# Twenty-four small score products of the compressed branch, handed out by threes

## The chip, the cores and the metric

The kernel runs on one core of a Trainium2 chip. The core has five engines with an instruction queue each: TensorE (PE in the rows; its weight loads are shown as PEld), VectorE (DVE), ScalarE (ACT), GpSimd (POOL) and SyncE (SP), which issues most transfers. Each engine takes its queue in order, and semaphores hold an instruction until what it needs is there. The metric is the time of one execution on the device in microseconds (us), the median over several runs.

## The reference

One layer of a decoder trunk for 256 tokens of width 2048, in float32. After a norm, one projection feeds three mixers: dilated window attention (12 heads, group "a"), block attention (8 heads, "b") and a sparse mixer (12 heads in 3 key groups, "c"). Their 32 head outputs go through an output projection and a residual; then a gated convolution FFN (width 5632) and a last norm. The change is in the sparse mixer's compressed branch, where each of the 12 heads scores 15 compressed keys:

```python
def chunk(c):
    ...
    s_c = jnp.einsum('bkgqe,bkne->bkgqn', qc, kc)
    p_c, _ = masked_softmax(s_c, cmp_end[None, :] <= t[:, None])
    o_c = jnp.einsum('bkgqn,bkne->bkgqe', p_c.astype(v_cmp.dtype), vc)
    ...
    return g[..., 0:1] * o_c + g[..., 1:2] * o_s + g[..., 2:3] * o_w
```

`o_s` and `o_w` are the selected and the window branch. With 256 tokens every block is selected, so both are causal attention over all keys, with keys and values of their own.

## The kernel before

**Main products.** Weights come from memory in chunks of 128 x 1024. ScalarE casts a chunk to a high part `wh` (L129), VectorE forms the rest `wl` (L131), and TensorE multiplies both with the split input: `wh` times 512 columns (L184), `wl` times 256 columns (L188). A chunk is 16 such main products. Raw chunks have 4 buffers, `wh` and `wl` 5 each. A unit of the projection (128 outputs, 32 main products, two chunks) fills one PSUM bank of the pool `mm`, which has three. When a unit is done, `evac` gathers it: ScalarE copies one half of the bank to `low` (L205), VectorE adds the other (L206), which frees the bank. `low` has one buffer (`FULL_BUFS = 1`); it is free again when the unit's outputs are written. For a query unit these are two query tiles (L346 on ScalarE, L347 on VectorE), and query tiles have 12 buffers.

**Order of the units.** First the twelve units of group c's keys and queries and its values (`cq0` to `cq5` are the queries, two heads each), then group a: `aq00, ak00, aq10, ak10, aq20, ak20`, then its values (three products to a piece, L406 to L408), and so on to group b. The six `cq` units fill all 12 query buffers.

**Side work.** The attention runs beside the main products as a list of Python generators. The main loop calls `step()` once after each chunk and twice after every second one; each call runs the first generator to its next `yield`. When `cq5` is issued, `c_attention` is started: first `cmp_attention` (the compressed branch), then `pipeline` over 24 head instances (12 heads, selected and window branch; the order is head 0, head 1 selected, head 0, head 1 window, then heads 2 and 3). One step of the pipeline turns an earlier instance's probabilities (three transposes, L585 to L587), scores one instance (three products, L532 and L534, into one of the two banks of the pool `sc`) and issues its softmax: a bias add (L546) and two reductions with a minimum (L548) on VectorE, which free the bank, two exponentials on ScalarE (L549), a factor (L552, L553, L557) and two scalings on VectorE (L580, L581). A query tile is free when both instances that use it are scored.

**The compressed branch** (L481 to L521): 12 products of 32 columns for each half of the tokens, into one `sc` bank each (L491); VectorE adds mask and low part (L493, L494), takes the minimum and subtracts it (L497, L498); ScalarE exponentiates (L500); then mask, sum, reciprocal, gate and scaling on VectorE (L503 to L511), and four transposes (L515, L516).

**The final order** on each engine is set when the program is built: a scheduler walks all instructions with a model of their durations, takes the ready one that stands earliest in the program's text, and hands out buffers. So the place of a `yield` sets which instructions stand earlier, and the built order is fixed for the chip.

Of the kernel before, what the change touches and what calls it, by code (L numbers as in the profile page):

```python
# [92 lines left out]
def trunk(ctx, tc, xT, wfm, wtm, wout, wup, wdown, wlast, gT, w1, w2, pe, relT, convp, onehot, maskc, cmask, vbmask, out, out_t):  # L93
# [115 lines left out]
    with tc.tile_pool(name="sc", bufs=2, space=bass.MemoryType.PSUM) as scp, \  # L209
# [107 lines left out]
        def turned(t):  # L317

            return t.rearrange("p (b c) -> p b c", c=P)[:, :, ::-1]
# [162 lines left out]
        def cmp_attention():  # L482
            ge = st["gate"].rearrange("p t g -> p (t g)")
            ps = ptp.tile([P, 512], F32, name="pt")
            T.matmul(ps[:, :72], flip, ge, start=True, stop=True)
            V.tensor_copy(ge, ps[:, :72])
            sm = rp.tile([P, 2, 12, 16], F32, name="sb")
            for tt in range(2):
                sps = scp.tile([P, 512], F32, name="sc")
                for h in range(12):  # L490
                    T.matmul(sps[:, h * 32:h * 32 + 32], qs[f"cq{h // 2}", h % 2][:, tt * P:(tt + 1) * P], cmp["k"][:, h // 4, :], start=True, stop=True)  # L491
                s3 = sps[:, :384].rearrange("p (h n) -> p h n", n=32)
                V.tensor_tensor(sm[:, tt], s3[:, :, :16], cm[:, 0, tt, :].unsqueeze(1).to_broadcast([P, 12, 16]), ALU.add)  # L493
                V.tensor_tensor(sm[:, tt], s3[:, :, 16:], sm[:, tt], ALU.add)  # L494
            sm2 = sm.rearrange("p t h n -> p (t h) n")
            mn = ap.tile([P, 24], F32, name="cmn")
            V.tensor_reduce(mn, sm2, AX.X, ALU.min)  # L497
            V.tensor_tensor(sm2, sm2, mn.unsqueeze(2).to_broadcast([P, 24, 16]), ALU.subtract)  # L498
            e = rp.tile([P, 2, 12, 16], F32, name="p", bufs=PROB_BUFS)
            A.activation(e, sm, AF.Exp, scale=-1.0)  # L500
            yield
            for tt in range(2):
                V.tensor_tensor(e[:, tt], e[:, tt], cm[:, 1, tt, :].unsqueeze(1).to_broadcast([P, 12, 16]), ALU.mult)  # L503
            e2 = e.rearrange("p t h n -> p (t h) n")
            den = ap.tile([P, 24], F32, name="cden")
            V.tensor_reduce(den, e2, AX.X, ALU.add)
            V.tensor_scalar_max(den, den, 1e-30)
            V.reciprocal(den, den)
            V.tensor_tensor(den.rearrange("p (t h) -> p t h", t=2), den.rearrange("p (t h) -> p t h", t=2),
                            st["gate"].rearrange("p t (h b) -> p t h b", b=3)[:, :, :, 0], ALU.mult)  # L510
            V.tensor_tensor(e2, e2, den.unsqueeze(2).to_broadcast([P, 24, 16]), ALU.mult)  # L511
            yield
            tp = ptp.tile([P, 512], F32, name="pt")
            for tt in range(2):
                T.transpose(tp[:, tt * P:(tt + 1) * P], e[:, tt, :8].rearrange("p h n -> p (h n)"), ident)  # L515
                T.transpose(tp[:64, 256 + tt * P:256 + (tt + 1) * P], e[:, tt, 8:].rearrange("p h n -> p (h n)"), ident)  # L516
            pc = cmp["pc"] = [cmp["big"][:, 6:8, :].rearrange("p a b -> p (a b)"), ap.tile([64, S], F32, name="pc1")]
            A.copy(pc[0].rearrange("p (b c) -> p b c", c=P), turned(tp[:, :S]))
            A.copy(pc[1].rearrange("p (b c) -> p b c", c=P), turned(tp[:64, S:2 * S]))
            yield  # L520
# [126 lines left out]
        def c_attention():  # L647
            insts = []
            for p in range(6):
                kv = p // 2  # L650
                for br, (grp, base) in enumerate((("s", 0), ("w", 192))):
                    for hf in range(2):
                        i = Inst(f"cq{p}", ("c", br, kv), "c", base + kv * HD, 20 + 2 * p + hf, grp, hf)
                        i.done = 10 + p if grp == "w" else None
                        insts.append(i)
            yield from cmp_attention()
            yield from pipeline(insts, 2, lambda j: scale(insts[j]))
# [335 lines left out]
```

## Time and profile before

| | us |
|---|---|
| median of 3 runs | 1161.84 (1161.62 to 1163.25) |
| the profiled execution | 1162.18 |
| its span in the profile | 1160.2 |
| TensorE busy | 1146.8 (99% of the span) |
| VectorE busy | 859.1 (74%) |
| ScalarE busy | 684.5 (59%) |
| granted TensorE clock, mean over the run | 0.998 of full speed |

The span runs from the first to the last instruction that the profile shows; the execution's time has 2.0 us around it. Busy shares are averages over stages with different limits: VectorE is far busier in the attention stage (the first 350 us) than later. A matmul's row shows its start and a modelled end, which overlaps the next one's start; how long it holds TensorE is read from start to start.

### The profile page before, as it was taken

The numbers are of one execution on the slowest core, as the hardware profiler recorded it, in microseconds if no ns is written. First come the engines' busy times: TensorE is split into PE (matmuls) and PEld (weight loads), VectorE is DVE, ScalarE is ACT, GpSimd is POOL, SyncE is SP. The second block draws the span as 40 slices with busy tenths as digits, with TensorE's granted clock in tenths as the row PEclk, the third lists the DMA queues.
The fourth block names the chain that finished last, engine by engine and source line by source line (L and its number), as shares of the span: only waits on it lengthen the run. The fifth ranks groups of instructions, "written<-read, shape, count | busy, mean of one in ns | idle before, by whom it ended". The sixth has DMA issues, their size and how long they took to land.

```text
span 1160.2 us, 18818 instructions
## 1 busy us (share of the span) xinstructions
PE 1146.8 (99%) x6931; PEld 1016.7 (88%) x6931; DVE 859.1 (74%) x1666; ACT 684.5 (59%) x1181; POOL 28.8 (2%) x61
## 2 busy tenths in 40 slices
PE   8999999999999999999999999999999999999997
PEld 6898998988888998888888888888888888888897
DVE  6877977877786878888888888888888555544565
ACT  7674786867764657655565555656556544444452
POOL 2000000100000000000000000000000100000000
PEclk9999999999999999999999999999999999999999
DMA  9765545565466755555555555555556866656612
GB/s 305 257 189 174 139 169 153 158 201 164 142 176 174 214 195 184 193 186 189 192 187 192 186 190 192 188 192 185 193 188 190 308 212 173 191 183 186 195 55 73
DMA packets 67276, 215.06 MB, mean 185 GB/s; under 512 B 7648, under 2 KB 11888, under 8 KB 67184
## 3 DMA queue, kind: packets, MB, share of 16 engines
q1 hardware_dynamic: 63200, 204.15, 54.7%
q0 software_dynamic: 3008, 8.86, 3.1%
q8 instruction: 55, 0.90, 0.3%
q10 hardware_dynamic: 976, 0.85, 0.2%
q14 instruction: 37, 0.30, 0.1%
HBM read 211.68 MB, written 2.15 MB: 184 GB/s over the span
## 4 chain that ended last, share of the span: by engine, by line
PE 98%; DMA 1%; DVE 0%; ACT 0%; SPq 0%; issue 0%; DVEq 0%
PE up L184 40%; PE up L188 21%; PE mm L184 13%; PE mm L188 6%; PE mm L407 2%; PE mm L406 2%; PE mm L408 2%; PE up L892 1%; PE up L894 1%; PE up L893 1%; PE sc L534 1%; PE o L611 1%; DMA gx<-in_xT_dram 1%; PE mm L195 1%; PE mm L193 1%; PE mm L194 1%
## 5 line engine op out<-in xcount | busy, mean ns | idle before, releaser
L131 DVE TENSOR_TENSOR wl<-raw,wh 128x1024 fp32r<-128x1024 f32 (+3 forms) x398 | 464.1, 1168 | 178.0 <-ACT wh L129 168.0
L129 ACT CAST wh<-raw 128x1024 fp32r<-128x1024 f32 (+3 forms) x398 | 400.5, 1008 | 263.2 <-PE up L184 177.4
L184 PE MATMUL up<-xx,wh 128*128 128x512 f32 x1408 | 483.8, 393 | 0.0
L188 PE MATMUL up<-xx,wl 128*128 128x256 f32 x1408 | 379.5, 280 | 0.0
L184 PEld LDWEIGHTS up<-xx,wh 128*128 128x128 f32 x1408 | 257.9, 188 | 50.9
L188 PEld LDWEIGHTS up<-xx,wl 128*128 128x128 f32 x1408 | 265.2, 188 | 7.9
L184 PE MATMUL up<-aa,wh 128*128 128x512 f32 x616 | 215.6, 394 | 0.0
L188 PE MATMUL up<-aa,wl 128*128 128x256 f32 x616 | 171.9, 283 | 0.0
L184 PE MATMUL mm<-xx,wh 128*128 128x512 f32 x448 | 158.6, 396 | 1.0 <-ACT wh L129 1.0
L184 PEld LDWEIGHTS up<-aa,wh 128*128 128x128 f32 x616 | 114.9, 188 | 25.4
L188 PE MATMUL mm<-xx,wl 128*128 128x256 f32 x448 | 122.9, 283 | 3.4 <-DVE wl L131 3.4
L188 PEld LDWEIGHTS up<-aa,wl 128*128 128x128 f32 x616 | 115.8, 188 | 1.2
L205 ACT COPY low<-up 128x256 f32<-128x256 f32 x88 | 32.8, 373 | 125.8 <-PE up L184 125.8
L184 PEld LDWEIGHTS mm<-xx,wh 128*128 128x128 f32 x448 | 82.9, 188 | 16.5 <-ACT wh L129 1.3
L188 PEld LDWEIGHTS mm<-xx,wl 128*128 128x128 f32 x448 | 84.3, 188 | 6.5 <-DVE wl L131 4.3
L206 DVE TENSOR_TENSOR low<-up,low 128x256 f32<-128x256 f32 x88 | 37.4, 425 | 55.8 <-ACT low L205 55.6
L184 PE MATMUL mm<-oo,wh 128*128 128x512 f32 x192 | 67.0, 395 | 0.0
L789 ACT ACTIVATE acc<-u,cw 128x256 f32<-128x256 f32 x88 | 53.2, 604 | 3.2 <-DVE u L787 0.6
L188 PE MATMUL mm<-oo,wl 128*128 128x256 f32 x192 | 52.1, 283 | 0.0
L407 PE MATMUL mm<-wh,xx 128*128 128x384 f32 (+2 forms) x128 | 46.3, 362 | 0.0
L406 PE MATMUL mm<-wh,xx 128*128 128x384 f32 (+2 forms) x128 | 46.3, 362 | 0.0
L408 PE MATMUL mm<-wl,xx 128*128 128x384 f32 (+2 forms) x128 | 45.5, 359 | 0.0
(250 smaller groups left out, 1305.8 us busy)
## 6 DMA issues: line engine op xcount, KB each, us to landing
raw<-in_wup_dram SPq DMA_DIRECT2D x176, 512.0 KB, 4.4
raw<-in_wdown_dram SPq DMA_DIRECT2D x70, 512.0 KB, 4.1
raw<-in_wfm_dram SPq DMA_DIRECT2D x62, 512.0 KB, 4.6
raw<-in_wo_dram SPq DMA_DIRECT2D x32, 384.0 KB, 3.1
raw<-in_wtm_dram SPq DMA_DIRECT2D x16, 384.0 KB, 3.3
bias<-table POOLq DMA_DIRECT2D x32, 128.0 KB, 3.8
raw<-in_wtm_dram SPq DMA_DIRECT2D x8, 512.0 KB, 4.5
raw<-in_wo_dram SPq DMA_DIRECT2D x8, 512.0 KB, 4.4
```

Of the source, the lines that this page charges most:

```text
L129: A.copy(wh[:, :n], raw[:, :n])
L131: V.tensor_tensor(wl[:, :n], raw[:, :n], wh[:, :n].bitcast(F32), ALU.subtract)
L184: T.matmul(ps, a, m.rearrange("p c s -> p (c s)"), start=start, stop=stop)
L188: T.matmul(ps[:, :S], b, m[:, 0, :], start=False, stop=False)
L193: T.matmul(ps[:, :S], a, m[:, 0, :], start=start, stop=False)
L194: T.matmul(ps[:, :S], a, m[:, 1, :], start=False, stop=False)
L205: A.copy(t, ps[:, S:])
L206: V.tensor_tensor(t, ps[:, :S], t, ALU.add)
L406: T.matmul(pss[tt][:, :n], xx[:, kt, 0, ts], a, start=kt == 0, stop=False)
L407: T.matmul(pss[tt][:, :n], xx[:, kt, 1, ts], a, start=False, stop=False)
L408: T.matmul(pss[tt][:, :n], xx[:, kt, 0, ts], b, start=False, stop=kt == NK - 1)
L789: A.activation(acc, u[:, 2:], AF.Identity, bias=cw[:, n, 3:4], scale=cw[:, n, 0:1])
```

## The change

Inside the loop over the 12 heads of a half, `cmp_attention` now yields after every third product. It had three yields before it ended and has eleven now, so each later step of `c_attention`, and of the generators behind it in the list, is run eight steps later.

```diff
                 for h in range(12):
                     T.matmul(sps[:, h * 32:h * 32 + 32], qs[f"cq{h // 2}", h % 2][:, tt * P:(tt + 1) * P], cmp["k"][:, h // 4, :], start=True, stop=True)
+                    if h % 3 == 2:
+                        yield
                 s3 = sps[:, :384].rearrange("p (h n) -> p h n", n=32)
```

The instructions are the same ones on every engine; the two added lines shift the line numbers behind L491 by two. The order on POOL and SP is the same. On TensorE, VectorE and ScalarE the order differs from the first small product to the scores of group b, about 900 main products further on.

TensorE's queue from the end of the first chunk of `aq00`. Before:

```order
L485 MATMUL pt<-gate,flip 128x72
L491 MATMUL sc<-kc,q 128x32 x20
L188 MATMUL mm<-xx,wl 128x256
...
L491 MATMUL sc<-kc,q 128x32 x4
L188 MATMUL mm<-xx,wl 128x256
```

and with the change:

```order
L485 MATMUL pt<-gate,flip 128x72
L491 MATMUL sc<-kc,q 128x32 x3
L188 MATMUL mm<-xx,wl 128x256
...
L491 MATMUL sc<-kc,q 128x32 x6
L184 MATMUL mm<-xx,wh 128x512
...
L491 MATMUL sc<-kc,q 128x32 x3
L188 MATMUL mm<-xx,wl 128x256
```

Before, 20 small products stand together and 4 more come 22 main products later. Now there are six groups (3, 6, 3, 6, 3, 3) with 16 main products between one and the next.

TensorE's queue around the end of `ak10`, the 112th main product after the first small one. `q_854` and `q_857` are the two query tiles of `cq0`, `q_909` and `q_912` those of `cq1`. Before, the first two scores (of `cq0`'s selected branch) stand 58 main products ahead of this place, and the next ones stand so (`mm_1505` is `ak10`, `mm_1643` is `aq20`):

```order
L532 MATMUL sc_1340<-k_545,q_854 128x256
...
L188 MATMUL mm_1505<-xx_83,wl_1378 128x256
L532 MATMUL sc_1404<-k_545,q_857 128x256
...
L515 MATMUL pt_1227<-ident_68,p_1195 128x128
...
L585 MATMUL pt_1334<-ident_68,p_1279 128x128
...
L184 MATMUL mm_1505<-xx_83,wh_1425 128x512
L532 MATMUL sc_1451<-k_510,q_909 128x256
...
L532 MATMUL sc_1476<-k_510,q_912 128x256
L534 MATMUL sc_1476<-k_510,q_912 128x256 x2
L184 MATMUL mm_1643<-xx_83,wh_1508 128x512
```

With the change all of them stand between `ak10` (`mm_1343`) and `aq20` (`mm_1441`):

```order
L184 MATMUL mm_1343<-xx_83,wh_1303 128x512
L534 MATMUL sc_1408<-k_510,q_854 128x256
...
L534 MATMUL sc_1464<-k_510,q_857 128x256
...
L534 MATMUL sc_1513<-k_545,q_854 128x256
...
L534 MATMUL sc_1540<-k_545,q_857 128x256
...
L534 MATMUL sc_1598<-k_510,q_909 128x256
...
L517 MATMUL pt_1396<-ident_68,p_1331 128x128
...
L587 MATMUL pt_1507<-ident_68,p_1415 128x128
...
L534 MATMUL sc_1645<-k_510,q_912 128x256
...
L184 MATMUL mm_1441<-xx_83,wh_1346 128x512
```

Six scores, the four transposes of the compressed branch and one turn (three transposes) now follow one another without a main product between them. Further on, after `ak20` (64 main products later), there is a second such row: four scores and three turns between `ak20` and the first product of group a's values.

VectorE's queue from the first of these scores' bias add to the gather of `ak00`. Before (`low_1359` is `ak00`'s gather):

```order
L546 TENSOR_TENSOR sb_1276<-sc_1272,bias_1268 128x128
...
L131 TENSOR_TENSOR wl_1559<-raw_1555,wh_1557 128x1024
...
L131 TENSOR_TENSOR wl_1648<-raw_1644,wh_1646 128x1024
...
L347 SCALAR_TENSOR_TENSOR q_1239<-low_1235,q_1239 64x256
...
L131 TENSOR_TENSOR wl_1695<-raw_1691,wh_1693 128x1024
L206 TENSOR_TENSOR low_1359<-mm_1245,low_1359 128x256
```

With the change (`low_1261` is `ak00`'s gather, whose end the first product of `aq20` waits for):

```order
L548 TENSOR_TENSOR sb_1412<-sc_1408,bias_1404 128x128
...
L131 TENSOR_TENSOR wl_1574<-raw_1570,wh_1572 128x768
...
L347 SCALAR_TENSOR_TENSOR q_1198<-low_1194,q_1198 64x256
...
L347 SCALAR_TENSOR_TENSOR q_1201<-low_1194,q_1201 64x256
...
L550 ISA sb_1544,nm_1545<-sc_1540,bias_1406 128x256
...
L206 TENSOR_TENSOR low_1261<-mm_1204,low_1261 128x256
```

The three chunk splits that stood between the first bias add and the gather of `ak00` are ahead of the bias add now, and the next split (768 wide) stands there instead. The bias adds and minima of four instances and the two query writes of `aq00` stand between them as before.

## Rows read from the trace of the kernel before

**Rows 1.** The page: TensorE's busy line, and the chain that ended last by engine

```profile
PE 1146.8 (99%) x6931; PEld 1016.7 (88%) x6931; DVE 859.1 (74%) x1666; ACT 684.5 (59%) x1181; POOL 28.8 (2%) x61
PE 98%; DMA 1%; DVE 0%; ACT 0%; SPq 0%; issue 0%; DVEq 0%
```

**Rows 2.** Busy us in one stretch: PE, PEld, DVE, ACT, POOL; clock, DMA share, GB/s

```profile
117.00:130.00 13.00, 13.00 (x85) 11.72 (x84) 12.48 (x45) 8.37 (x22) 1.08 (x2) 1.00 0.46 136
```

**Rows 3.** Waits of ScalarE from 116 to 160: total us, times, longest

```profile
ACT q L346 <- PE sc L534: 2.0, 4, 0.7
```

**Rows 4.** Timeline, TensorE, the small products: start us, duration us, instruction

```profile
104.82 2.38 PE L491 MATMUL sc<-kc,q 128*128 128x32 f32 x20
...
110.99 0.51 PE L491 MATMUL sc<-kc,q 128*128 128x32 f32 x4
...
111.35 0.36 PE L188 MATMUL mm<-xx,wl 128*128 128x256 f32 x1
```

**Rows 5.** Timeline, TensorE, the first scores, transposes and the start of `aq20`

```profile
117.01 0.28 PE L532 MATMUL sc<-k,q 128*128 128x256 f32 x1
...
117.72 0.28 PE L188 MATMUL mm<-xx,wl 128*128 128x256 f32 x1
...
123.65 0.28 PE L532 MATMUL sc<-k,q 128*128 128x256 f32 x1
...
128.39 0.27 PE L585 MATMUL pt<-ident,p 128*128 128x128 f32 x1
128.50 0.27 PE L586 MATMUL pt<-ident,p 128*128 128x128 f32 x1
...
130.34 0.39 PE L184 MATMUL mm<-xx,wh 128*128 128x512 f32 x1
```

**Rows 6.** Timeline, ScalarE, a query write and a gather's copy

```profile
124.20 0.42 ACT L346 ACTIVATE q<-low 64x256 fp32r<-64x256 f32 x1 [0.70 <-PE sc L534]
...
127.14 0.37 ACT L205 COPY low<-mm 128x256 f32<-128x256 f32 x1
```

**Rows 7.** Timeline, VectorE, from the first bias add to `ak00`'s gather

```profile
118.39 0.28 DVE L546 TENSOR_TENSOR sb<-sc,bias 128x128 f32<-128x128 f32 x1
118.59 0.61 DVE L503 TENSOR_TENSOR p<-p,cm 128x192 f32<-128x192 f32 x2
...
120.97 1.22 DVE L131 TENSOR_TENSOR wl<-raw,wh 128x1024 fp32r<-128x1024 f32 x1
122.10 0.30 DVE L508 RECIPROCAL cden<-cden 128x24 f32<-128x24 f32 x1
...
125.14 0.28 DVE L580 TENSOR_SCALAR p<-p,f 128x128 f32<-128x128 f32 x1
...
125.59 0.28 DVE L546 TENSOR_TENSOR sb<-sc,bias 128x128 f32<-128x128 f32 x1
125.91 0.42 DVE L347 SCALAR_TENSOR_TENSOR q<-low,q 64x256 fp32r<-64x256 f32 x1
...
129.39 0.42 DVE L206 TENSOR_TENSOR low<-mm,low 128x256 f32<-128x256 f32 x1
```

**Rows 8.** Timeline, VectorE, from a later bias add to the gathers of `ak10` and `aq20`

```profile
138.03 0.28 DVE L546 TENSOR_TENSOR sb<-sc,bias 128x128 f32<-128x128 f32 x1
...
141.81 0.94 DVE L131 TENSOR_TENSOR wl<-raw,wh 128x768 fp32r<-128x768 f32 x1
142.66 0.29 DVE L548 CUSTOM_DVE_ANT_0 sb<-sc,sb 128x128 f32<-128x128 f32 x1
...
143.29 0.42 DVE L206 TENSOR_TENSOR low<-mm,low 128x256 f32<-128x256 f32 x1
...
148.22 0.42 DVE L206 TENSOR_TENSOR low<-mm,low 128x256 f32<-128x256 f32 x1 [0.30 <-ACT low L205]
```

**Rows 9.** Busy time in two stretches with TensorE mostly idle (columns as in Rows 2)

```profile
10.00:12.00 2.00, 0.53 (x3) 0.19 (x1) 0.79 (x2) 1.73 (x3) 0.00 (x0) 1.00 1.02 392
1153.00:1156.00 3.00, 0.49 (x2) 0.30 (x2) 2.54 (x9) 0.20 (x1) 0.00 (x0) 0.79 0.16 54
```

## The prediction, made before the changed kernel ran

> **What bounds the kernel now.** I read the page first: the reader is to see that TensorE is busy 99% of the span and that the chain that ended last runs through it for 98% [rows 1]. So time that TensorE gains or loses in the middle of the program moves the end by as much, unless something later gives it back. I read the stretch around the edit next, by engine: TensorE is busy for all of its 13.00 us, and VectorE for 12.48 of them [rows 2]. There VectorE has next to no room, and whatever TensorE must wait for on VectorE will take the full length of VectorE's queue. The waits name the place: ScalarE already waits four times, 2.0 us in all, for scores before it can write group a's query tiles [rows 3], since the twelve query buffers hold group c's queries until these are scored. Last I read the timelines of the three engines for durations.
>
> **What the change moves.** The number of instructions stays. The small products come apart, and every later step of the attention comes eight steps later. The main loop calls three steps for two chunks, so that is 16/3 chunks or some 15 us (32 main products, two chunks, took 5.66: 111.35 to 117.01) [rows 4, 5]. The unit `aq00` can't write its queries, and `low` stays taken, until `cq0`'s four scores are done; `ak00` can't be gathered until `low` is free; and with three `mm` banks, `aq20` has none until `ak00` is gathered. Before, `ak00`'s gather starts at 129.39 and takes 0.42, and `aq20`'s first product starts at 130.34: 0.53 us of room [rows 5, 7]. Eight steps are far more. The built order shows it: the scores of `cq0` now stand behind the last product that has a bank, and TensorE must run six scores, four transposes and a turn in a row, at VectorE's pace, before `aq20`.
>
> **The small products.** Twenty took 2.38, 0.119 each with the modelled end, and the group of four took 0.36 until the next main product, 0.09 each [rows 4]: the first weight load of a group lies under the main product ahead of it, the others don't. There are four groups more, so I take 4 x 0.09 = 0.36 off, rounded to -0.3. The bounds: if all 24 loads hid and the products cost nothing, -2.7 (2.38 + 0.36); if breaking the row cost as much as it saves, +0.3.
>
> [...]
>
> **The first stall** (between `ak10` and `aq20`). Four pieces of TensorE's own work lie in it and are needed anyway, so they are no loss: two scores take 0.71 (117.01 to 117.72), so a score takes 0.355 and six take 2.13; a transpose takes 0.11 (128.39 to 128.50), so four and three take 0.77 [rows 5]. Sum 2.90.
>
> Its length is VectorE's queue. From a score's start to the next engine's start there passed 0.55 (123.65 to 124.20, an idle ScalarE that waited for it) [rows 5, 6]. Then VectorE runs everything from the first bias add to the end of `ak00`'s gather. Before, the same stretch ran from 118.39 to 129.39 + 0.42 = 129.81: 11.42 us [rows 7]. Of what lay in it, the new stretch lacks three chunk splits of 1.13 (120.97 to 122.10; there are three such), the two mask products (0.61), one of the two scalings (125.14 to 125.59, 0.45) and a small factor (0.1); it has one split of 768 columns more (141.81 to 142.66, 0.85) [rows 7, 8]. So 11.42 - 3.39 - 0.61 - 0.45 - 0.1 + 0.85 = 7.72. With the 0.55 the stretch takes 8.27; less 2.90 of work, TensorE idles 5.37.
>
> **The second stall** (between `ak20` and group a's values). The same chain one turn later: `cq1`'s last two scores stand here, `aq10`'s queries wait for them, and `ak10`'s gather waits for `low`. TensorE's own work: four scores 1.42 and three turns 0.99 = 2.41. VectorE's queue from the bias add of the first score to the gather of `ak10`: before, a stretch of the same make-up ran from 138.03 to 143.29 + 0.42 = 143.71, 5.68 us, with one split of 768 columns too many (0.85); the new one has a bias add (0.2, 118.39 to 118.59) and two small factors (0.1 each) more [rows 7, 8]. 5.68 - 0.85 + 0.4 = 5.23. With the 0.55: 5.78; less 2.41, idle 3.37.
>
> The next handover, `aq20`'s bank for the second half of group a's values, comes after 30 products of those values (5.3 us at 5.66/32 each, with the scores among them more) and needs the next gather, which came 4.93 us behind `ak10`'s (143.29 to 148.22) [rows 8]: I count nothing there. From there on the attention is 9 us late and the main products are 9 us late too, so VectorE has the same time for it as before.
>
> **Bounds of the two stalls.** From below, by dependence alone, as if VectorE's queue were empty otherwise: score to bias add 0.55; bias add 0.2 and minima 0.63 (142.66 to 143.29), twice 0.83 for two instances; the last score 0.55, query write 0.42 on ScalarE and 0.42 on VectorE, copy 0.37, gather 0.42 [rows 6 to 8]: 4.39, less 2.90, idle 1.5. The second: 0.55, two query writes 0.84, 0.42, 0.37, 0.42 = 2.60, less 2.41, idle 0.2. Together 1.7. From above, if TensorE's work in them gave nothing back elsewhere, 8.27 + 5.78 = 14.1. I take 5.37 + 3.37 = 8.7, since the rows of VectorE's own queue are the nearest: it was busy for 96% of that stretch.
>
> **The sum.** 8.7 - 0.3 = 8.4. The profiled execution took 1162.18, its span 1160.2 and 2.0 around it; with the change 1170.6. It is 0.34 above the median of the runs shown, so on that scale 1161.84 + 8.4 = **1170.2**.
>
> **Rivals.** *The clock falls in the stalls.* [...] If the clock falls, the main products behind a stall run at half speed until it rises. I price it by the 32 products of `aq20`: their 5.66 double at half speed; that is nothing to 5.7 for each stall, and I take half of it for the first one: 1170.2 + 2.8 = 1173.
>
> [...]
>
> *A third handover stalls too.* VectorE is the engine at its limit, and group c's softmax now starts later and must end at the same place. If `aq20`'s gather, or a chunk split behind it, is late by the length of one softmax and one split (0.83 + 1.13) or two, the time is 1170.2 + 2 to 4 = 1172 to 1174.
>
> *Not slower.* One mechanism would do it: VectorE runs the moved work while it would have idled, so that the stalls shrink to their dependence (1.7), and the spread small products hide their loads (-2.7): 1161.84 - 1.0 = 1160.8. It decides where both stalls come to 2.7 together: with 0.2 for the second, VectorE's queue from the first bias add to `ak00`'s gather would take 2.90 + 2.5 - 0.55 = 4.85 instead of 7.72. Against it: 12.48 of 13.00 [rows 2], and that the built order puts that work on VectorE ahead of the gather. Half-way cases (a stall of half the length) give 1164 to 1167.
>
> That the change doesn't do what it says is out: the built order has the six groups.
>
> **How the numbers follow.** The forecast of two stalls with the clock up, 0.55; its own range is 1168 to 1172.5. The clock, 0.20; a third stall, 0.10; stalls of half the length, 0.11; not slower, 0.04. The range that leaves two in ten out is 1166.5 to 1177: below it lie the not-slower case and part of the half-length ones, above it both stalls with the clock down and a third one. A measurement of this kernel tells about 0.2% (2.3 us) from no change. Slower by more than that: all cases but the last and a sliver of the half-length ones, 0.95; within, 0.03; faster, 0.02.
>
> **What would show it.** TensorE's gaps in the changed profile: scores of the first row 1.2 to 1.6 us apart instead of 0.36, `aq20`'s first product starting about 8.3 us after the first score, and the first product of group a's values about 5.8 us after the end of `ak20`; the releaser named for these waits should be VectorE, with the gather (L206) last. Busy TensorE in all should stay and its idle time grow by about 9. Everything behind the second stall should run as before, shifted. If the gaps are there but the end moves less, something later gave time back and my reading of the end is wrong. If TensorE's queue is dense around `aq20`, the chain of buffers is wrong. If the clock row shows less than 1.00 behind the stalls, the first rival holds.

## The result and the profile after

| | before | changed |
|---|---|---|
| median | 1162.08 us (4 runs, 1161.62 to 1163.25) | 1175.24 us (4 runs, 1174.48 to 1175.32) |
| span of the profiled execution | 1160.2 | 1173.2 |
| TensorE busy | 1146.8 | 1154.8 |
| granted clock, mean | 0.998 | 0.994 |

The changed kernel is slower: ratio 1.0103, 95% interval 1.0091 to 1.0114, so +12.0 us (10.6 to 13.2). The medians of the table lie 13.2 us apart and the spans of the two profiled executions 13.0, where +8.4 was forecast. The traces are held against the 13.0, the runs below against each other by their ratios. The time lies inside the range (1166.5 to 1177) and outside the forecast's own one (1168 to 1172.5).

The page of the changed kernel, the lines of [rows 1]:

```profile
PE 1154.8 (98%) x6931; PEld 1021.7 (87%) x6931; DVE 861.7 (73%) x1666; ACT 684.8 (58%) x1181; POOL 28.8 (2%) x61
...
PE 97%; DVE 1%; DMA 1%; ACT 1%; SPq 0%; issue 0%; DVEq 0%; ACTq 0%
```

TensorE's instructions are the same in number, yet it is "busy" 8.0 us longer. Part of that is the clock, the new thing here: the same product is drawn longer where the clock is lower (0.63 us against 0.39, below). The stretches from 127 to 159 us, columns as in [rows 2]:

```profile
127.00:136.00 9.00, 5.53 (x27) 4.52 (x26) 8.59 (x42) 4.75 (x15) 1.07 (x2) 0.72 0.39 105
136.00:138.00 2.00, 2.00 (x9) 1.81 (x8) 0.73 (x3) 1.95 (x6) 0.00 (x0) 0.54 0.34 66
138.00:150.00 12.00, 12.00 (x76) 10.66 (x76) 8.87 (x35) 8.13 (x22) 0.00 (x0) 1.00 0.34 91
150.00:155.00 5.00, 2.44 (x15) 1.60 (x13) 4.76 (x22) 4.00 (x15) 1.19 (x2) 0.99 0.51 155
155.00:159.00 4.00, 4.00 (x16) 4.00 (x15) 3.67 (x19) 3.47 (x12) 0.00 (x0) 0.58 0.20 31
159.00:170.00 11.00, 11.00 (x68) 10.19 (x66) 7.60 (x29) 7.07 (x17) 1.07 (x2) 1.00 0.23 55
```

Two stretches with TensorE half empty and VectorE full (8.59 of 9.00, 4.76 of 5.00) are the two stalls. The granted clock falls below 1.00 in and behind the first and behind the second: TensorE is fully busy from 136 to 138 and from 155 to 159, and gets 0.54 and 0.58 of its speed. A busy share alone would hide that.

The waits of TensorE between 100 and 420 us (total, times, longest); before there was none from 100 to 300:

```profile
PE sc L534 <- DVE f L559: 2.3, 1, 2.3
PE sc L534 <- DVE nm L550: 1.3, 1, 1.3
PE sc L534 <- DVE f L554: 0.9, 1, 0.9
PE sc L534 <- DVE cden L511: 0.7, 1, 0.7
PE pt L517 <- DVE f L555: 0.5, 1, 0.5
PE mm L406 <- DVE low L206: 0.2, 1, 0.2
```

Each ends on VectorE. The instruction that is named came last by time; for a score it is the minimum (L550) that frees its bank, and the small factors and `cden` stand beside it in VectorE's queue. The first product of `aq20` has no wait of its own here (see the account below). The same two stalls in TensorE's timeline, which answers to [rows 5]: the row of six scores, four transposes and a turn ahead of `aq20`, then the row behind `ak20` up to group a's values (the last line is the second of these products):

```profile
127.27 0.28 PE L534 MATMUL sc<-k,q 128*128 128x256 f32 x1
...
129.47 0.36 PE L534 MATMUL sc<-k,q 128*128 128x256 f32 x1 [1.33 <-DVE nm L550]
...
130.97 0.50 PE L534 MATMUL sc<-k,q 128*128 128x256 f32 x1 [0.91 <-DVE f L554]
...
132.64 0.55 PE L534 MATMUL sc<-k,q 128*128 128x256 f32 x1 [0.73 <-DVE cden L511]
...
134.13 0.45 PE L517 MATMUL pt<-ident,p 128*128 128x128 f32 x1 [0.50 <-DVE f L555]
...
136.29 0.63 PE L184 MATMUL mm<-xx,wh 128*128 128x512 f32 x1
...
148.80 0.28 PE L534 MATMUL sc<-k,q 128*128 128x256 f32 x1
...
153.32 0.36 PE L534 MATMUL sc<-k,q 128*128 128x256 f32 x1 [2.26 <-DVE f L559]
...
154.66 0.49 PE L406 MATMUL mm<-wh,xx 128*128 128x384 f32 x1 [0.15 <-DVE low L206]
154.94 0.52 PE L407 MATMUL mm<-wh,xx 128*128 128x384 f32 x1
```

The first row takes 136.29 - 127.27 = 9.02 us (8.27 forecast), the second 154.66 - 148.80 = 5.86 (5.78 forecast). The lengths of single matmuls show the clock: a main product of 512 columns is drawn with 0.63 at 136.29, at the start of the stretch with 0.54, where it had 0.39 in [rows 5]. And VectorE's queue, the bias adds and the gathers of the two rows, which answer to [rows 7, 8]:

```profile
127.82 0.29 DVE L548 TENSOR_TENSOR sb<-sc,bias 128x128 f32<-128x128 f32 x1 [0.29 <-PE sc L536]
...
134.97 0.42 DVE L206 TENSOR_TENSOR low<-mm,low 128x256 f32<-128x256 f32 x1
...
149.36 0.29 DVE L548 TENSOR_TENSOR sb<-sc,bias 128x128 f32<-128x128 f32 x1 [0.19 <-PE sc L536]
...
154.20 0.40 DVE L206 TENSOR_TENSOR low<-mm,low 128x256 f32<-128x256 f32 x1
```

From the first bias add to the gather's end VectorE needs 135.39 - 127.82 = 7.57 (7.72 forecast) and 154.60 - 149.36 = 5.24 (5.23 forecast).

### The profile page after: what moved, and what is told of

Its sections match the earlier page's. It is cut to its first block, busy times and chain, and to the rows that moved or that the text cites. A ratio compares the mean times of both kernels' runs of the same rounds, so it can differ in the third digit from the quotient of the medians.

```text
span 1173.2 us, 18821 instructions
## 1 busy us (share of the span) xinstructions
PE 1154.8 (98%) x6931; PEld 1021.7 (87%) x6931; DVE 861.7 (73%) x1666; ACT 684.8 (58%) x1181; POOL 28.8 (2%) x61
## 4 chain that ended last, share of the span: by engine, by line
PE 97%; DVE 1%; DMA 1%; ACT 1%; SPq 0%; issue 0%; DVEq 0%; ACTq 0%
PE up L184 40%; PE up L188 20%; PE mm L184 13%; PE mm L188 6%; PE mm L406 2%; PE mm L407 2%; PE mm L408 2%; PE up L894 1%; PE up L896 1%; PE up L895 1%; PE sc L536 1%; DMA gx<-in_xT_dram 1%; PE pt L613 1%; PE o L613 1%; PE mm L195 1%; PE mm L193 1%
## 5 line engine op out<-in xcount | busy, mean ns | idle before, releaser
L131 DVE TENSOR_TENSOR wl<-raw,wh 128x1024 fp32r<-128x1024 f32 (+3 forms) x398 | 463.9, 1168 | 183.9 <-ACT wh L129 174.3
```

What stands on the lines that cost most here:

```text
L131: V.tensor_tensor(wl[:, :n], raw[:, :n], wh[:, :n].bitcast(F32), ALU.subtract)
```

## The experiments

The theory after the result: the delay of eight steps, not the breaking up of the row, makes two stalls as long as VectorE's queue, by way of query tiles, `low` and banks; the clock falls in them and costs more on top. The rivals: interleaving costs in itself; VectorE is late whatever the buffers; the loss grows with the delay step by step; the clock does not matter. Line numbers below are those of each kernel.

**The delay alone.** The kernel before, with eight empty steps, and all small products in a row:

```diff
             sm = rp.tile([P, 2, 12, 16], F32, name="sb")
+            for _ in range(8):
+                yield
             for tt in range(2):
```

> The kernel before, with eight empty steps ahead of the 24 small products, which stay in a row: the delay alone. If the delay of the attention makes the loss (two stalls of TensorE at VectorE's pace between ak10 and aq20 and between ak20 and group a's values, and the lower clock behind them), the time is that of the changed kernel: before + 13.0 us, between +11.5 and +14, with the clock at 0.50 for some 7 us from 131 on and some 3.5 us from 155 on. If the breaking up of the row costs, by more weight loads in the open or by groups that wait on banks, this kernel is much nearer to before: +0 to +4.

Measured: 1175.28 us, ratio 1.0109 (1.0094 to 1.0124), +12.7 us: the changed kernel's loss. The delay makes it. One part came out otherwise: in the profiled execution (1173.91, the fastest of four) the clock fell in the first stall alone. Its stretches, columns as above:

```profile
136.00:138.00 2.00, 2.00 (x8) 1.71 (x8) 1.82 (x11) 1.92 (x6) 0.00 (x0) 0.50 0.33 59
...
155.00:159.00 4.00, 4.00 (x26) 3.97 (x24) 3.62 (x17) 3.18 (x11) 0.00 (x0) 1.00 0.13 23
```

**The threes alone.** While small products are out, the main loop steps after every four main products (it steps after sixteen otherwise), so the attention isn't late:

```diff
-                products(ps, wq.get(), 8, 8 * c, xx, c == 0, c == 1)
...
+                    products(ps, part, 2, 8 * c + i, xx, (c, i) == (0, 0), (c, i) == (1, 6))
+                    yield
...
-                        yield
+                        yield "more"
...
+                if kind == "f" and more[-1]:
+                    step()
...
+                        if ticks % 2 == 0:
+                            step()
```

> The changed kernel, but while the small products are handed out the main loop takes a step after every four main products instead of after every sixteen, so that they come by threes (in groups of 1 to 6) and the first score stands 52 main products behind the first small one instead of 112 (54 before). By the theory of the delay the stalls are gone: no row of scores, clock 1.00, and only the broken row is left: before + 0.2, between -0.3 and +0.8. By the theory that interleaving costs in itself: +4 or more.

Measured: 1162.19 us, ratio 0.9994 (0.9986 to 1.0003), and TensorE waits nowhere between 100 and 300 us. Breaking up the row costs nothing that can be measured, and saves nothing either.

**A second `low` buffer**, the delay kept:

```diff
-FULL_BUFS, KEY_BUFS, QUERY_BUFS, PROB_BUFS = 1, 9, 12, 12
+FULL_BUFS, KEY_BUFS, QUERY_BUFS, PROB_BUFS = 2, 9, 12, 12
```

> The changed kernel with two buffers for the gathered half (FULL_BUFS 2 instead of 1): the delay stays, one link of the chain query tile - gathered half - bank of main products is opened. If the chain is what I said, ak00 is gathered while aq00 waits for its query tiles, aq20 has a bank in time, and the scores stand between main products: before + 0.5, between 0 and +2, clock 1.00. If the stall comes from VectorE being late with the attention whatever the buffers (VectorE as the bound), the loss stays: +9 to +13.

Measured: 1162.63 us, ratio 0.9998 (0.9990 to 1.0007). The stretch that held both stalls, columns as above:

```profile
120.00:160.00 40.00, 40.00 (x251) 37.67 (x250) 35.65 (x129) 29.56 (x77) 2.15 (x4) 1.00 0.48 134
```

One buffer of 1 KB a partition takes the whole loss back, with the eight steps of delay still in. VectorE is busy for 35.65 of the 40 us and TensorE waits for nothing, so VectorE had time for the work; what held TensorE was that the work stood ahead of its next bank.

**TensorE kept busy in the stalls**, by products that nothing reads, issued behind the named instances' scores:

```diff
+FILL = {1: 10, 2: 7, 3: 8, 4: 7, 8: 16}
...
+                with tc.issue_after(done.ins):
+                    for _ in range(FILL[n.i]):
+                        T.matmul(o[:, :S], xx[:, 0, 0, :P], xx[:, 0, 0, :], start=True, stop=True)
```

> The changed kernel with products that nothing reads, each like a main product of 256 columns (0.12 us), in TensorE's gaps: 32 in the first row of scores, 16 in the second (the order of scores and turns around the second row changes a little with it). If the lower clock costs 3.4 us of the 13.0 (0.85 by transposes and a score at half speed at the end of the first stall, 0.8 by aq20's products, 1.8 by the first products of group a's values), the clock stays at 1.00 and the time is before + 9.6, between +8.5 and +10.5. If the clock costs nothing that matters, or the gaps are not what brings it down: +13 or more, since the fillers can only delay.

Measured: 1170.04 us, ratio 1.0063 (1.0050 to 1.0075), +7.3 us where +9.6 was expected: 5 us faster than the changed kernel by doing more work. The clock stays at 1.00, and the first row, with 32 fillers in it, is shorter. Two stretches, then TensorE's timeline at the first score, at `aq20` and around the second row (columns as above):

```profile
127.00:136.00 9.00, 8.65 (x63) 7.55 (x62) 8.59 (x42) 5.25 (x16) 1.07 (x2) 1.00 0.40 106
...
155.00:159.00 4.00, 4.00 (x29) 4.00 (x28) 2.12 (x12) 2.61 (x11) 0.00 (x0) 1.00 0.00 0
```

```profile
127.02 0.28 PE L535 MATMUL sc<-k,q 128*128 128x256 f32 x1
...
127.73 1.34 PE L542 MATMUL o<-xx 128*128 128x256 f32 x10
...
135.19 0.50 PE L185 MATMUL mm<-xx,wh 128*128 128x512 f32 x1
...
147.41 0.28 PE L535 MATMUL sc<-k,q 128*128 128x256 f32 x1
...
151.24 0.44 PE L407 MATMUL mm<-wh,xx 128*128 128x384 f32 x1 [0.39 <-DVE low L207]
```

135.19 - 127.02 = 8.17 us: the 8.27 of the prediction. So 0.85 of the changed kernel's 9.02 was the clock. Its own trace agrees: there the gather of `ak00` ended at 135.39 and `aq20` started 0.90 later, when TensorE's transposes and last score were through at the low clock; with the fillers `aq20` starts as the gather ends. The 5 us are more than the 3.4 I expected of the clock, because the fillers also changed the built order: the second row now holds two scores and two turns instead of four and three, and takes 3.83 us, of which 1.37 are TensorE's own work (two scores 0.71, two turns 0.66), so it idles 2.46 instead of 3.45. Some 4 us are left for the clock.

**The second stall filled alone** (`FILL = {8: 16}`), which leaves the order ahead of it as it was:

> The changed kernel with 16 products of 256 columns that nothing reads in the second row alone, where TensorE idles 2.26 us; everything up to it in the changed kernel's order. The first stall and its half-speed stretch stay. If the lower clock behind the second stall costs 1.8 us (3.6 us of group a's value products at half speed), the clock is 1.00 from 155 on and the time is before + 11.2, between +10.5 and +12. If the fillers only delay: +13 or more.

Measured: 1173.99 us, ratio 1.0091 (1.0077 to 1.0104), by the ratios some 1.4 us less than the changed kernel's. The first stall has its low clock, the second not:

```profile
131.00:138.00 7.00, 5.35 (x20) 4.65 (x21) 5.98 (x30) 4.00 (x13) 1.08 (x2) 0.53 0.39 89
...
155.00:159.00 4.00, 3.90 (x22) 3.90 (x23) 3.74 (x21) 3.89 (x12) 0.00 (x0) 1.00 0.21 48
```

The gain is near the 1.8 expected; the intervals of the two ratios overlap, so the row on the clock shows it better than the times.

**Four steps and two steps late.** A yield after every sixth small product:

```diff
-                    if h % 3 == 2:
+                    if h % 6 == 5:
```

> The changed kernel with a yield after every sixth small product instead of every third: four steps late instead of eight. In the built order the first two scores now stand among ak10's products, and ahead of aq20 there are four scores and two turns in a row. By the method of the prediction VectorE's queue from the first of these bias adds to ak00's gather has two instances' bias adds and minima 1.66, two query writes 0.9, one split 1.13, a scaling 0.45 and small factors 0.9, with 0.55 in front 5.6; less 2.1 of TensorE's own work, idle 3.5. Behind ak20 no such row stands. So before + 3.5, between +2 and +6. A loss in proportion to the delay would be half of 13.0: +6.5. If the stalls start only with the full eight steps: +0 to +1.

and one behind every twelfth (`if h == 11:`):

> The changed kernel with one yield behind each half's twelve products: two steps late. Ahead of aq20 stand two scores and a turn, as before, and 26 to 32 main products lie between most scores. By the theory of the buffers (a stall only where cq0's scores move behind the last product that has a bank) before + 0.5, between 0 and +1.5. In proportion to the delay: +3.3. By the room of 0.53 us that I read from ak00's gather to aq20's first product, with two steps worth 3.8 us: a stall of some 3 us.

Measured: four steps 1167.23 us, ratio 1.0029 (1.0018 to 1.0039), so +3.4 (+2.1 to +4.5); two steps 1162.39, ratio 0.9993 (0.9984 to 1.0002). Neither is in proportion to the loss of eight steps (6.0 and 3.0 of its 12.0). With four steps TensorE waits in a single row ahead of `aq20`, and the clock stays at 1.00 from 126 to 162:

```profile
131.85 0.30 PE L587 MATMUL pt<-ident,p 128*128 128x128 f32 x1 [1.31 <-DVE p L582]
132.60 0.33 PE L588 MATMUL pt<-ident,p 128*128 128x128 f32 x1 [0.45 <-DVE p L583]
...
133.24 0.36 PE L534 MATMUL sc<-k,q 128*128 128x256 f32 x1 [0.20 <-DVE f L554]
```

With two steps the first score comes no later than before (117.01):

```profile
116.12 0.28 PE L534 MATMUL sc<-k,q 128*128 128x256 f32 x1
```

The main loop hands out one or two steps at a time, and a step falls where its chunk ends. My count of 15 us for eight steps must not be divided by eight, and it was too long: the eight steps moved the first score by 10.3 us (117.01 to 127.27).

**VectorE's queue shortened.** The compressed branch's sum, reciprocal, gate and scaling are left out:

```diff
-            V.tensor_reduce(den, e2, AX.X, ALU.add)
...
-            V.tensor_tensor(e2, e2, den.unsqueeze(2).to_broadcast([P, 24, 16]), ALU.mult)
```

> The changed kernel without the compressed branch's sum, reciprocal, gate and scaling (L508 to L513, which stand on VectorE between the first scores' bias adds; they hold it 1.44 us: 0.46, 0.08, 0.32, 0.10 and 0.48 from start to start in the changed kernel's trace); its probabilities stay unscaled. If VectorE's queue sets the length of the first stall, the stretch from the first score to aq20's first product falls from 9.02 by 1.44 or more, to about 7.5, and the time to before + 11.5, between +10 and +12. If the chain of dependences sets it (scores, minima, query tiles, gather), or the lower clock, the length stays: +13.

Measured: 1173.47 us, ratio 1.0085 (1.0072 to 1.0099), +9.9 us. The first row, from its first score to `aq20`:

```profile
127.01 0.28 PE L527 MATMUL sc<-k,q 128*128 128x256 f32 x1
...
134.57 0.63 PE L184 MATMUL mm<-xx,wh 128*128 128x512 f32 x1
```

7.56 us: the 1.44 us that VectorE lost came off the 9.02 one for one (7.58). The four transposes moved to the head of the row with it, so the order isn't quite the same. In this row a microsecond on VectorE is a microsecond of TensorE. The time came out at +9.9 (8.4 to 11.5 by the interval), where I expected +11.5, counted from 13.0. By the ratios it fell by 2.1 from the changed kernel's 12.0, and the two intervals overlap, so what goes beyond the row's 1.46 can't be told from noise.

**More query tiles instead of a second `low`.** 14 of them, paid for with a probability tile:

```diff
-FULL_BUFS, KEY_BUFS, QUERY_BUFS, PROB_BUFS = 1, 9, 12, 12
+FULL_BUFS, KEY_BUFS, QUERY_BUFS, PROB_BUFS = 1, 9, 14, 11
```

> The changed kernel with 14 query tiles instead of 12, paid for with one probability tile (11 instead of 12). It opens the first link of the chain: aq00 can write its queries while cq0's scores are still out. If the chain starts there, no row of scores stands between ak10 and aq20, the clock stays at 1.00 and the time is before + 0.5, between -0.5 and +2. If the one buffer for the gathered half alone makes the stall, or VectorE is simply late, the loss stays: +9 to +13.

Measured: 1167.10 us, ratio 1.0031 (1.0019 to 1.0043). Half right: neither old stall is there, but a third row of scores stands later, behind group c's first values, with a low clock (columns as above; total, times, longest):

```profile
200.00:220.00 20.00, 16.80 (x110) 14.37 (x109) 14.55 (x67) 14.01 (x44) 1.67 (x4) 0.91 0.28 71
```

```profile
PE sc L534 <- DVE nm L550: 2.4, 1, 2.4
...
PE sc L534 <- DVE f L559: 0.8, 1, 0.8
```

I had not expected it. To see whether the missing probability tile makes it, the same 14 query tiles were paid for with a bias tile:

```diff
-            t = rp.tile([P, 2 * P], F32, name="bias", bufs=3)
+            t = rp.tile([P, 2 * P], F32, name="bias", bufs=2)
```

> As the run with 14 query tiles, but paid for with one bias tile (2 instead of 3) and all 12 probability tiles kept. If the late row of scores around 205 us (3.2 us idle, clock 0.91 in 200 to 220) came from the missing probability tile, it is gone and the time is before + 0.5. If it belongs to the order that comes with 14 query tiles, it is there again: before + 3.6, between +2.5 and +5.

Measured: 1167.62 us, ratio 1.0040 (1.0026 to 1.0054), with the same two waits of 2.4 and 0.8. So the probability tile isn't its cause; the late row comes with the order that 14 query tiles bring. Why the scheduler puts that row there wasn't traced.

**A second `low` in the kernel before:**

> The kernel before with two buffers for the gathered half. TensorE has no wait between 100 and 300 us there, so a second buffer has nothing to give: before + 0, between -1 and +1. If the kernel before loses time in the same chain without showing a wait (by an order that the scheduler bends around it), it is faster by 1 to 3 us.

Measured: 1163.75 us, ratio 1.0006 (0.9997 to 1.0015). Nothing: the buffer is worth the whole loss or none of it, by whether the attention is late. No kernel of this study is faster than the kernel before by more than the measurement tells.

## Why the prediction was right in sign and too small

- *The chain of buffers* was right. The delay alone makes the loss, and opening the chain at `low` takes it back; opening it at the query tiles removes these two stalls as well.
- *The length of the stalls* was right. VectorE's queue took 7.57 and 5.24 us where 7.72 and 5.23 were forecast, and 1.44 us less work on VectorE made the first row 1.46 shorter. It was this stretch that was full, not the attention stage as a whole: before, VectorE is busy for 275.92 of the first 350 us (0.79) and for 583.20 of the 810.20 behind them (0.72). Of 9.02 and 5.86 us, 2.90 and 2.41 are TensorE's own work: 6.12 and 3.45 lost, against 5.37 and 3.37; without the 0.85 of the clock the first is 5.27.
- *The clock* is the step that failed. The forecast let the main products behind a stall run at full speed and gave the rival 0.20. The changed kernel's clock fell in the first stall and behind the second. By rows: 0.85 in the first row (9.02 against 8.17 with fillers); (1 - 0.54) x 2 = 0.9 from 136 to 138, of which 0.15 lies still in the row, so 0.8; (1 - 0.58) x 4 = 1.7 from 155 to 159; in sum 3.4. That is less than the rival's price (2.8 a stall; 5.6 for both would make 1170.2 + 5.6 = 1175.8). That 1175.8 lies so near the 1175.24 measured is in part luck, since the 5.6 for the clock covers 3.4 of clock, the 0.3 that the small products didn't save, and time that isn't assigned to anything. No row ahead of the prediction shows the rival's half speed: [rows 9] has one stretch of 2 us that kept the clock and one of 3 us with a mean of 0.79, and neither is evidence for stalls of 8 and 6 us. In shorter stretches that end of the kernel before does show it (columns as in [rows 2]):

```profile
1154.00:1154.50 0.50, 0.44 (x2) 0.30 (x2) 0.46 (x2) 0.00 (x0) 0.00 (x0) 1.00 0.00 0
1154.50:1155.00 0.50, 0.05 (x1) 0.00 (x0) 0.44 (x3) 0.00 (x0) 0.00 (x0) 0.71 0.00 0
1155.00:1155.50 0.50, 0.00 (x0) 0.00 (x0) 0.50 (x3) 0.00 (x0) 0.00 (x0) 0.50 0.14 51
```

  The changed kernel has 0.50 from 131 to 137 and from 155 to 158, and 1.00 again from 138 and from 159 on. The second stall of the kernel with the empty steps (clock 1.00) and the single row of the one with four steps (waits of 1.31, 0.45 and 0.20, clock 1.00) show that the fall needn't happen.
- *The small products* saved nothing, where 0.3 was forecast. From the first group to the last, 105.02 to 121.38, lie 21 of them and 80 main products:

```profile
105.02 0.49 PE L491 MATMUL sc<-kc,q 128*128 128x32 f32 x3
...
121.38 0.40 PE L491 MATMUL sc<-kc,q 128*128 128x32 f32 x3
```

  In the kernel before, behind its last small product [rows 4]:

```profile
111.55 0.40 PE L184 MATMUL mm<-xx,wh 128*128 128x512 f32 x1
...
111.79 0.28 PE L188 MATMUL mm<-xx,wl 128*128 128x256 f32 x1
111.91 0.39 PE L184 MATMUL mm<-xx,wh 128*128 128x512 f32 x1
...
115.61 0.28 PE L188 MATMUL mm<-xx,wl 128*128 128x256 f32 x1
```

  22 main products with nothing between them take 3.82 us there (111.79 to 115.61), 0.174 each. By that rate 80 take 13.9 of the 16.36 us, so 21 small ones cost 2.5, and 24 would cost 2.8. Before, 24 small ones and 24 main products took 6.97 (104.82 to 111.79), of which 4.2 are the main products: 2.8 again. The prediction counted a group only up to the next main product. That one then held TensorE 0.20 us (111.35 to 111.55), where its like takes 0.12 (111.79 to 111.91), and 0.20 also behind the twenty (107.06 to 107.26) and behind the changed kernel's first three (105.36 to 105.56): what these groups save at the head they pay behind their end.
- *The sum*, as measured: lost in the two rows 6.12 + 3.45 (the 0.85 of the clock is in the first), 0.8 + 1.7 behind them at the low clock, nothing for the small products: 12.1 of the 13.0 by which the span grew. Of the last 0.9, 0.2 was there before the change acts (the first small product starts at 105.02, before at 104.82); 0.7 is not assigned.
- *A third handover* did not stall in the changed kernel: behind 155 there is no wait of TensorE up to 420. *Not slower* was out: VectorE had the 7.57, not 4.85.
- *What would show it*: in the first row the scores came 0.35, 1.85, 1.50, 1.67 and 2.86 us apart (the last with seven transposes between), where 1.2 to 1.6 was said; the releaser is VectorE throughout. The gather came last at the second row's end (the wait of 0.15), but not at the first's, where TensorE's own work at the low clock ended 0.90 after it. That busy TensorE would stay and its idle time grow by 9 was wrong in form: busy grew by 8.0 and idle by 5.0, since a slow matmul counts as busy, and so does the modelled end of one that an idle time follows: of the first row's 9.02 us TensorE is drawn busy for 5.54, where its own work and the clock make 2.90 + 0.85.

## What to carry to other kernels

A yield added to cooperative side work is a delay for everything behind it; ask which buffers that work gives back, and walk the chain from them to the next bank of the engine that bounds the kernel. Price such a stall as the full queue of the engine that must give the buffer back, in its built order (7.57 and 5.24 us here), and give the half-speed time behind a long row a large chance: here the clock fell to 0.50 in and behind the changed kernel's first row and behind its second, and stayed at 1.00 behind the second row of the kernel with the empty steps. Before reordering, try one more buffer at the narrowest link: here 1 KB a partition was worth the whole loss. And count small work inserted among large from one large product to a later one of the same kind, since here part of its cost showed in the next large product (0.20 us against 0.12).

## What the runs showed that I had not expected

Work that nothing reads made the kernel 5 us faster: with it in the gaps TensorE's clock was 1.00 from 127 to 136, where the changed kernel had 0.72. The clock isn't settled by a stall's shape alone: the row behind `ak20`, with the same 2.26 us of idle time at the same place, was followed by a clock of 0.58 in the changed kernel and of 1.00 in the one with eight empty steps. Its wait and first value product there:

```profile
153.02 0.35 PE L534 MATMUL sc<-k,q 128*128 128x256 f32 x1 [2.26 <-DVE f L559]
...
154.35 0.44 PE L406 MATMUL mm<-wh,xx 128*128 128x384 f32 x1 [0.15 <-DVE low L206]
```

What decides between the two was not found.
